# Other order of products, earlier block sums and stores on another queue in the up projections of a hybrid decoder trunk

## The chip, the cores and the metric

The kernel runs on one core of a Trainium2 chip. Its engines are TensorE (PE, matmuls; PEld is its weight load), VectorE (DVE), ScalarE (ACT), GpSimd (POOL) and SyncE (SP, which only issues DMAs here). Each engine takes its instructions in program order and waits at the first one that is not ready; DMAs are issued in that order as well, from SP's or ScalarE's queue. The metric is device microseconds of one execution, the median of three runs. The profile is one execution taken by the hardware profiler.

## What is computed

A trunk of two layers on 1024 tokens of width 1024, in float32. Layer 0 mixes with an S5 state space model and gated linear attention, layer 1 with an xLSTM matrix memory. Each mixer is followed by a gated MLP with a causal convolution of width 3, and the change lies in that MLP:

```python
def conv_ffn(h, w_up, conv_w, conv_b, w_down):
    g, u = jnp.split(h @ w_up, 2, axis=-1)          # 1024 -> 2 x 2816
    g = causal_dwconv(g, conv_w, conv_b)
    return ((jax.nn.gelu(g, approximate=True) * u) @ w_down).astype(h.dtype)

# per layer
x = x + rms_norm(mix, ln_mix_post[layer])
h = rms_norm(x, ln_ffn_pre[layer])
f = conv_ffn(h, ffn_w_up[layer], ffn_conv_w[layer], ffn_conv_b[layer], ffn_w_down[layer])
x = x + rms_norm(f, ln_ffn_post[layer])
```

## The kernel before, in words

Every large product is made in three matmuls: each operand is cut into a rounded part h (ScalarE copies it into the fast 32-bit format) and the remainder l (DVE subtracts), and TensorE adds hh, hl and lh (`cut`, `mm3`). Matmuls have 512 columns. A "product" below is one 512 x 128 output tile over half of the depth: 4 depth tiles x 3 matmuls = 12 matmuls.

The up projection works in 22 pairs j: 128 columns of g and the 128 columns of u beside them, for all 1024 tokens in two halves, lo and hi. Each pair is a 2 x 2 block product with 7 products instead of 8 (a Winograd form). Two of them ("11" and "21", `up_first`) need the lo tokens only and the plain weight block a (of g). Five (`up_pair`) need sums of weight blocks and the block sums T1 to T4 and "22" of the activations, which `prenorm_blocks` makes from both halves, in four steps c of transposes, DVE, ScalarE and POOL work. While the hi half is still being normed, the first `EARLY` = 10 pairs run `up_first` alone (the early loop of `ffn`); they store g and u of the lo half to DRAM in `first` and load them again later (`outputs`). So there are ten early pairs with 5 products left (60 matmuls) and twelve whole pairs with 7 (84 matmuls). Pair 0 is the first one after the early loop.

The weights come through `Stream`, a list of units. A unit loads raw blocks on SP's queue (tags wr for a, wq for b, three buffers each), makes its tensor and cuts it. `next` gives the weights of the next unit, `advance` cuts units up to two ahead and loads further ones if buffers are free; `hold` keeps it from loading wq blocks until the early loop is over. `up_units` lists them per pair: for a whole pair first the plain a, then "sums" (POOL makes four sums of 512 columns: d = a1 - b1, b1 += b2, a1 = b1 - a1, a2 -= a1, and a is cut), then b, then d. Products of a pair come as T2 (first half of the sums), T1 and T4 (b), 22 (second half of the sums), T3 (d).

After a pair, `gate` makes the convolution (first tap on POOL, two more taps on DVE) and GELU (ScalarE); `late`, called after T2 of the next pair, multiplies with u on DVE and stores the product to `md` on SP, then issues the loads of the next outputs. `od_prep` prepares the odd layer's block matrices in the background during layer 0's MLP (POOL, TensorE transposes, ScalarE copies). Background tasks are put between the matmuls by `tick`, which keeps a planned time per lane; `finish` puts the rest of a task at once. The order of instructions on each engine is the order of the program.

Of the kernel before, what the change touches and what calls it, by code (L numbers as in the profile page):

```python
# [8 lines left out]
F32 = mybir.dt.float32  # L9
# [16 lines left out]
class Unit:  # L26
# [4 lines left out]
    def __init__(self, loads, make=None, state=None, done=("a",), keep=0):  # L31
        self.loads, self.make, self.done, self.keep = loads, make, done, keep
        self.state = {} if state is None else state

# [5 lines left out]
class Stream:  # L40
# [29 lines left out]
    def _cut(self):  # L70
        u = self.units[self.n_cut]
        r = u.make(self.k, u.state)
# [17 lines left out]
    LOOK = 3  # L90

# [88 lines left out]
class Trunk:  # L180
# [157 lines left out]
    def prenorm_blocks(self, xt, ss, gain, layer, base, out):  # L338
# [21 lines left out]
        for c in range(4):  # L360
# [17 lines left out]
            V.tensor_tensor(out=t34[:, 1], in0=t12[:, 1], in1=h2, op=ALU.subtract)  # L378
            G.tensor_tensor(out=t34[:, 1], in0=t34[:, 1], in1=l2, op=ALU.subtract)
# [123 lines left out]
    EARLY = 10  # L503

    def up_units(self, w, pairs, early):

        def col(c0):  # L510
            return w[:, c0 : c0 + 128].rearrange("(k p) c -> p k c", p=128)

        def sums(k, s):
            G = k.nc.gpsimd
            k.ws.live["wq"] += 1
            s["d"] = k.ws.raw([128, 4, 128], "wq")
            (a1, a2), (b1, b2) = ((s[n][:, 0:4], s[n][:, 4:8]) for n in "ab")
            G.tensor_tensor(out=s["d"], in0=a1, in1=b1, op=ALU.subtract)
            G.tensor_tensor(out=b1, in0=b1, in1=b2, op=ALU.add)
            G.tensor_tensor(out=a1, in0=b1, in1=a1, op=ALU.subtract)  # L520
            G.tensor_tensor(out=a2, in0=a2, in1=a1, op=ALU.subtract)
            return s["a"]

        units = [plain(col(c0)) for c0, _ in pairs[:early]]
        for i, (c0, c1) in enumerate(pairs):
            s, a, b = {}, ("a", col(c0)), ("b", col(c1))
            if i >= early:
                units.append(Unit([a], lambda k, s: s["a"], s, ()))
            units += [
                Unit([b] if i >= early else [a, b], sums, s, ("a",), 1),  # L530
                Unit([], lambda k, s: s["b"], s, ("b",)),
                Unit([], lambda k, s: s["d"], s, ("d",)),
            ]
        return units
# [9 lines left out]

    def up_first(self, B, g, u):
# [4 lines left out]
        p = self.up_product(w, 1, B["21"])  # L550
        self.nc.vector.tensor_tensor(out=g, in0=u, in1=p, op=ALU.add)

    def up_pair(self, B, g, u, late):

        lo, hi = slice(0, HT), slice(HT, 2 * HT)
        product = self.up_product

        def acc(o, i, ps, op=ALU.add):
            self.nc.vector.tensor_tensor(out=o, in0=i, in1=ps, op=op)

        wa = self.ws.next()
        acc(u[:, lo], u[:, lo], product(wa, 0, B["T2"]))
        late()
        wb = self.ws.next()
        acc(u[:, hi], u[:, lo], product(wb, 0, B["T1"]))
        acc(u[:, lo], u[:, lo], product(wb, 1, B["T4"]), ALU.subtract)
        acc(g[:, hi], u[:, hi], product(wa, 1, B["22"]))
        p = product(self.ws.next(), 0, B["T3"])
        acc(u[:, hi], u[:, hi], p)
        acc(u[:, lo], u[:, lo], p)  # L570
# [103 lines left out]
    def ffn(self, layer, src, hT, nxt):  # L674
# [4 lines left out]
        B = {"11": hT[0][0][:4], "21": hT[0][0][4:]}  # L679
        for j in range(self.EARLY):  # L680
            st = self.ws.raw([128, 2, HT], "wq")
            self.up_first(B, st[:, 0], st[:, 1])
            nc.sync.dma_start(out=self.first[j], in_=st)
        self.hold = False
# [4 lines left out]
        def gate(j, g):  # L689
# [20 lines left out]
        pend = None  # L710
# [16 lines left out]
        for j in range(NF):  # L727
            g, u = nxt_out
            if j >= self.EARLY:
                self.up_first(B, g[:, lo], u[:, lo])  # L730
            if j + 1 == NF:
                self.mids_load(1)
            self.up_pair(B, g, u, late)
# [3 lines left out]
        product()  # L737

# [872 lines left out]
    def od_prep(self):  # L1611
# [15 lines left out]
        gout = pre.tile([128, self.NT, 8], F32, name="gout")  # L1627
        yield 60000
        for c2 in range(8):
# [13 lines left out]
            for i in range(3):  # L1643
# [3 lines left out]
                o = pre.tile([128, 2, 128], F32, tag=f"bt{i}", name=f"bt{i}")  # L1647
# [17 lines left out]
            nc.vector.tensor_copy(gout[:, cs], pg[:, 0])  # L1665
# [4 lines left out]
        nc.sync.dma_start(out=self.gxd, in_=gout)  # L1670
# [592 lines left out]
```

## Time and profile before

| | us |
|---|---|
| median of 3 runs | 2810.51 (2805.34 to 2813.19) |
| profiled execution | 2813.47 |
| its span, first to last instruction | 2811.5 |
| TensorE busy | 2651.5 (94%) |
| VectorE busy | 1699.8 (60%) |
| ScalarE busy | 1042.5 (37%) |
| GpSimd busy | 777.0 (28%) |

The profile's page gives busy time by engine, and a slice table with the clock that TensorE was granted (PEclk, 1.00 is the full 2.4 GHz). A matmul's shown duration includes the fill of the array, so matmuls overlap: the distance from one start to the next is what one costs. The timeline lists instructions in order of time with, in brackets, how long the engine had been idle and what ended it. The windows view gives busy time per engine, number of instructions, clock and DMA share for a stretch.

### The profile page before, as it was taken

The page shows a single profiled execution, that of the slowest core. Times are in us where ns is not written, and L with a number is a line of the kernel's source. Part 1 is how long each engine was busy: PE and PEld are TensorE (multiplying, and loading weights), DVE is VectorE, ACT ScalarE, POOL GpSimd, SP SyncE. Part 2 cuts the span into 40 slices and gives each one's busy share as a digit, 9 for nine tenths or more (in the row PEclk, how much of TensorE's full clock was granted, in tenths as well). Part 3 has the DMA queues.
Part 4 walks back from the last instruction along what each step waited for, and adds up shares of the span by engine and source line. Part 5 has one row for each costly group of instructions (what it writes and reads, how often), then busy time and mean ns, then how long its engine had stood idle before and what let it go on. Part 6 is the DMA issues. An engine that isn't in the chain of part 4 may idle for free. (4 is left out here: it accounts for less than half of the span.)

```text
span 2811.5 us, 34544 instructions
## 1 busy us (share of the span) xinstructions
PE 2651.5 (94%) x13102; PEld 2193.7 (78%) x13102; DVE 1699.8 (60%) x2333; ACT 1042.5 (37%) x1580; POOL 777.0 (28%) x763
## 2 busy tenths in 40 slices
PE   6899899799999999999999999999997999999997
PEld 5676678677788788878788799998785777878886
DVE  7576456767656644377266467764556776666453
ACT  4233644422222333355344544433433222223331
POOL 2832003455343101020000035550113643330021
PEclk9999999899999999999999999999998999999999
DMA  5544446434232455265445534435444342325552
GB/s 139 151 132 128 139 139 190 155 107 145 80 98 71 147 183 202 91 200 157 135 146 157 177 122 141 135 101 194 167 169 138 120 135 75 90 68 202 180 194 75
DMA packets 413682, 392.10 MB, mean 139 GB/s; under 512 B 57902, under 2 KB 319624, under 8 KB 413388
## 3 DMA queue, kind: packets, MB, share of 16 engines
q1 hardware_dynamic: 374268, 354.69, 39.9%
q10 hardware_dynamic: 39248, 35.20, 3.6%
q8 instruction: 103, 1.69, 0.2%
q14 instruction: 63, 0.52, 0.1%
HBM read 288.96 MB, written 98.78 MB: 138 GB/s over the span
## 5 line engine op out<-in xcount | busy, mean ns | idle before, releaser
L118 DVE TENSOR_TENSOR wl<-wr,wh 128x1024 fp32r<-128x1024 f32 (+1 forms) x323 | 405.2, 1256 | 669.2 <-ACT wh L118 657.5
L134 PE MATMUL ps<-hh,wh 128*128 128x512 f32 x1876 | 750.2, 400 | 19.1 <-ACT wh L118 14.9
L134 PE MATMUL ps<-hh,wl 128*128 128x512 f32 x1876 | 742.8, 396 | 13.4 <-DVE wl L118 11.2
L134 PE MATMUL ps<-hl,wh 128*128 128x512 f32 x1876 | 739.1, 394 | 0.9 <-DVE hl L118 0.9
L118 ACT ACTIVATE wh<-wr 128x1024 fp32r<-128x1024 f32 (+1 forms) x326 | 338.9, 1041 | 699.3 <-PE ps L134 476.0
L134 PEld LDWEIGHTS ps<-hh,wl 128*128 128x128 f32 x1876 | 355.4, 189 | 106.3 <-DVE wl L118 28.0
L134 PEld LDWEIGHTS ps<-hh,wh 128*128 128x128 f32 x1876 | 356.5, 190 | 103.1 <-ACT wh L118 18.4
L134 PE MATMUL ps<-wh,hh 128*128 128x512 f32 x1076 | 423.9, 394 | 2.9 <-ACT hh L118 1.7
L134 PE MATMUL ps<-wh,hl 128*128 128x512 f32 x1076 | 420.1, 390 | 1.6 <-DVE hl L118 1.6
L134 PE MATMUL ps<-wl,hh 128*128 128x512 f32 x1076 | 419.9, 390 | 0.8 <-DVE wl L118 0.8
L134 PEld LDWEIGHTS ps<-hl,wh 128*128 128x128 f32 x1876 | 356.5, 190 | 74.7 <-DVE hl L118 1.4
L134 PEld LDWEIGHTS ps<-wh,hh 128*128 128x128 f32 x1076 | 202.6, 188 | 47.5 <-ACT hh L118 2.8
L134 PEld LDWEIGHTS ps<-wh,hl 128*128 128x128 f32 x1076 | 202.5, 188 | 45.5 <-DVE hl L118 2.9
L134 PEld LDWEIGHTS ps<-wl,hh 128*128 128x128 f32 x1076 | 202.7, 188 | 42.2 <-DVE wl L118 1.1
L118 POOL TENSOR_TENSOR rsp<-ms,mhalf 128x4 f32<-128x4 f32 x8 | 8.1, 1014 | 564.1 <-DVE ms L118 564.1
L118 DVE TENSOR_TENSOR wl<-wq,wh 128x1024 fp32r<-128x1024 f32 x88 | 107.4, 1220 | 88.5 <-ACT wh L118 88.5
L118 ACT ACTIVATE xs<-xs 128x1024 f32<-128x1024 f32 x44 | 46.7, 1062 | 258.8 <-DVE xs L118 212.5
L118 DVE TENSOR_TENSOR ys<-ys,ps 128x512 f32<-128x512 f32 x207 | 137.6, 681 | 4.6 <-PE ps L134 3.2
L118 POOL TENSOR_SCALAR xs<-xs,par_t 128x256 f32<-128x256 f32 (+1 forms) x96 | 100.9, 1061 | 118.1 <-DVE xs L118 118.1
L118 DVE SCALAR_TENSOR_TENSOR xs<-xs,par_t 128x1023 f32<-128x1023 f32 x88 | 126.9, 1442 | 1.6
L118 POOL TENSOR_TENSOR wq<-wr,wq 128x512 f32<-128x512 f32 x44 | 59.2, 1346 | 200.7 <-DVE wl L118 149.5
L118 POOL TENSOR_TENSOR wr<-wq,wr 128x512 f32<-128x512 f32 x44 | 67.4, 1533 | 105.4 <-DVE wl L118 103.7
(394 smaller groups left out, 4039.7 us busy)
## 6 DMA issues: line engine op xcount, KB each, us to landing
wr<-in_ffn_w_down_dram SPq DMA_DIRECT2D x88, 512.0 KB, 3.7
wr<-in_ffn_w_up_dram SPq DMA_DIRECT2D x64, 512.0 KB, 4.8
wr<-in_od_w_in_dram SPq DMA_DIRECT2D x64, 512.0 KB, 3.9
wq<-in_ffn_w_up_dram SPq DMA_DIRECT2D x44, 512.0 KB, 5.7
md<-xs SPq DMA_DIRECT2D x44, 512.0 KB, 2.9
wq<-md SPq DMA_DIRECT2D x44, 512.0 KB, 4.8
wr<-in_od_w_out_dram SPq DMA_DIRECT2D x32, 512.0 KB, 3.6
wr<-in_ev_w_in_dram SPq DMA_DIRECT2D x28, 512.0 KB, 4.2
```

Source lines behind the costliest of these rows:

```text
L118: return f(*args, **kw)
L134: self.eng.matmul(out=out, lhsT=lhsT, rhs=rhs, start=start, stop=stop)
```

## The change

The order of the five products becomes T2, T3 (both with d), T1, T4 (both with b), 22 (with a2); T3 and T4 change sign in `prenorm_blocks`. The sums tile d now holds both a1 - b1 and b1 + b2 - a1 in a wq buffer of its own; three POOL sums come ahead of its cut and the fourth (a2) gets a unit of its own, `last`. A unit may be marked `ahead`: `prepare`, called after the T3 product and once in the early loop, loads and sums the next pair's blocks before their cut is due. `EARLY` is 14. The early loop keeps its results in two tiles `su` and `sg` of one buffer each and stores them from ScalarE's queue, `hold` is cleared ahead of it. In `gate` the first tap moves from POOL to ScalarE, and the store of the product of the pair before is issued there from ScalarE's queue instead of SP's. `od_prep` uses one tile less and shares two tags.

```diff
+    def prepare(self):
+        for n in range(self.n_cut, min(self.n_cut + 4, len(self.units))):
+            u = self.units[n]
+            if u.ahead and u.made is None:
+                while self.n_dma <= n:
+                    self._load(True)
+                u.made = u.make(self.k, u.state)
+                return
...
-    EARLY = 10
+    EARLY = 14
...
         def sums(k, s):
             G = k.nc.gpsimd
             k.ws.live["wq"] += 1
-            s["d"] = k.ws.raw([128, 4, 128], "wq")
-            (a1, a2), (b1, b2) = ((s[n][:, 0:4], s[n][:, 4:8]) for n in "ab")
-            G.tensor_tensor(out=s["d"], in0=a1, in1=b1, op=ALU.subtract)
+            d = s["d"] = k.ws.raw([128, 8, 128], "wq")
+            a1, b1, b2 = s["a"][:, 0:4], s["b"][:, 0:4], s["b"][:, 4:8]
+            G.tensor_tensor(out=d[:, 4:8], in0=a1, in1=b1, op=ALU.subtract)
             G.tensor_tensor(out=b1, in0=b1, in1=b2, op=ALU.add)
-            G.tensor_tensor(out=a1, in0=b1, in1=a1, op=ALU.subtract)
-            G.tensor_tensor(out=a2, in0=a2, in1=a1, op=ALU.subtract)
-            return s["a"]
+            G.tensor_tensor(out=d[:, 0:4], in0=b1, in1=a1, op=ALU.subtract)
+            return d
+
+        def last(k, s):
+            a2 = s["a"][:, 4:8]
+            k.nc.gpsimd.tensor_tensor(out=a2, in0=a2, in1=s["d"][:, 0:4], op=ALU.subtract)
+            return a2
...
-                Unit([b] if i >= early else [a, b], sums, s, ("a",), 1),
+                Unit([b] if i >= early else [a, b], sums, s, (), 1, True),
                 Unit([], lambda k, s: s["b"], s, ("b",)),
-                Unit([], lambda k, s: s["d"], s, ("d",)),
+                Unit([], last, s, ("a", "d")),
...
+        if whole:
+            acc(g[:, lo], u[:, lo], self.up_first(B, u[:, lo]))
+        w = self.ws.next()
+        acc(g[:, hi], u[:, lo], product(w, 0, B["T2"]))
+        p = product(w, 1, B["T3"])
+        self.ws.prepare()
+        acc(u[:, lo], g[:, hi], p)
         late()
+        w = self.ws.next()
+        p = product(w, 0, B["T1"])
+        acc(u[:, hi], u[:, lo], p)
+        acc(g[:, hi], g[:, hi], p)
+        acc(u[:, lo], u[:, lo], product(w, 1, B["T4"]))
+        acc(g[:, hi], g[:, hi], product(self.ws.next(), 0, B["22"]))
...
+        self.hold, before = False, None
+
+        def put(i, n, t):
+            nc.scalar.dma_start(out=self.first[i, :, n], in_=t)
+
         for j in range(self.EARLY):
-            st = self.ws.raw([128, 2, HT], "wq")
-            self.up_first(B, st[:, 0], st[:, 1])
-            nc.sync.dma_start(out=self.first[j], in_=st)
-        self.hold = False
+            u = self.fpool.tile([128, HT], F32, tag="su", name="su", bufs=1)
+            p = self.up_first(B, u)
+            if before:
+                put(j - 1, 0, before)
+            put(j, 1, u)
+            before = self.fpool.tile([128, HT], F32, tag="sg", name="sg", bufs=1)
+            nc.vector.tensor_tensor(out=before, in0=u, in1=p, op=ALU.add)
+            if j + 2 == self.EARLY:
+                self.ws.prepare()
+        put(j, 0, before)
...
-            nc.gpsimd.tensor_scalar(
-                out=tt, in0=g, scalar1=w[2], scalar2=self.par("ffn_conv_b", layer * NF + j), op0=ALU.mult, op1=ALU.add
+            nc.scalar.activation(
+                out=tt, in_=g, func=AF.Identity, scale=w[2], bias=self.par("ffn_conv_b", layer * NF + j)
             )
...
+            if done:
+                nc.scalar.dma_start(out=self.md[done[0] * 128 : (done[0] + 1) * 128], in_=done.pop())
+                done.clear()
             nc.scalar.activation(out=tt, in_=tt, func=AF.Gelu_apprx_tanh)
...
-            nc.sync.dma_start(out=self.md[i * 128 : (i + 1) * 128], in_=tt)
+            done.extend((i, tt))
```

## Rows read from the trace of the kernel before

**Rows 1.** The page, busy time of each engine over the whole span.

```profile
PE 2651.5 (94%) x13102; PEld 2193.7 (78%) x13102; DVE 1699.8 (60%) x2333; ACT 1042.5 (37%) x1580; POOL 777.0 (28%) x763
```

**Rows 2.** Windows, layer 1: early loop, pair 0, pairs 1 to 9, pairs 10 to 21.

```profile
core 0: us, PE busy (x) PEld busy (x) DVE busy (x) ACT busy (x) POOL busy (x), PEclk, DMA share, GB/s
2083.36:2146.92 63.56, 58.15 (x273) 48.27 (x271) 43.07 (x44) 27.72 (x42) 24.70 (x14) 0.99 0.45 158
2146.92:2178.65 31.73, 19.72 (x61) 14.21 (x61) 25.26 (x25) 11.88 (x15) 13.64 (x9) 0.64 0.42 133
2178.65:2317.21 138.56, 129.76 (x542) 102.17 (x540) 105.32 (x107) 32.54 (x36) 75.64 (x44) 0.98 0.41 125
2317.21:2555.87 238.66, 232.40 (x1010) 188.18 (x1008) 162.72 (x172) 65.31 (x76) 77.79 (x59) 1.00 0.30 91
```

**Rows 3.** Windows, layer 0: the same four stretches.

```profile
472.93:537.48 64.55, 58.83 (x273) 48.56 (x272) 45.14 (x46) 27.69 (x42) 26.97 (x17) 0.98 0.57 164
537.48:570.03 32.55, 21.75 (x82) 16.70 (x83) 24.30 (x23) 12.70 (x18) 18.73 (x13) 0.67 0.41 133
570.03:712.31 142.28, 135.69 (x607) 110.25 (x606) 106.77 (x115) 36.53 (x49) 82.79 (x54) 0.98 0.42 130
712.31:962.00 249.69, 243.24 (x1098) 198.86 (x1096) 159.21 (x178) 70.06 (x92) 86.91 (x69) 0.99 0.30 91
```

**Rows 4.** Windows, layer 1, single pairs: two early ones (1 and 6), a whole one.

```profile
2178.65:2192.25 13.60, 13.60 (x62) 11.26 (x60) 10.52 (x11) 4.88 (x5) 8.11 (x5) 1.00 0.12 40
2252.56:2269.10 16.54, 14.25 (x61) 10.92 (x59) 11.15 (x13) 2.69 (x4) 8.44 (x5) 1.00 0.57 177
2378.51:2398.21 19.70, 19.34 (x86) 15.69 (x84) 13.40 (x14) 5.12 (x7) 6.71 (x6) 1.00 0.28 81
```

**Rows 5.** Timeline, layer 1, ahead of pair 0: SP, POOL, ACT, PE; start, duration.

```profile
2111.62 19.87 SPq L683 DMA_DIRECT2D first<-wq  x4
2132.06 0.93 SPq L65 DMA_DIRECT2D wq<-in_ffn_w_up_dram  x1
...
2138.50 1.29 POOL L118 TENSOR_TENSOR wq<-wr,wq 128x512 f32<-128x512 f32 x1 [6.84 <-DMA wq<-in_ffn_w_up_dram]
...
2142.57 1.26 POOL L118 TENSOR_TENSOR wr<-wr 128x512 f32<-128x512 f32 x1
...
2143.86 1.06 ACT L118 ACTIVATE wh<-wr 128x1024 fp32r<-128x1024 f32 x1 [15.10 <-POOL wr L118]
...
2146.92 0.80 PE L134 MATMUL g<-hh,wh 128*128 128x512 f32 x1 [5.41 <-ACT wq L118]
2147.51 0.63 PE L134 MATMUL g<-hl,wh 128*128 128x512 f32 x1
```

**Rows 6.** Timeline, layer 1: transposes of blocks 0 and 1, last cut of block 0.

```profile
2111.92 0.60 PE L138 MATMUL ps<-ident,x 128*128 128x128 f32 x4
...
2123.01 1.04 PE L138 MATMUL ps<-ident,x 128*128 128x128 f32 x8
...
2121.96 1.23 DVE L118 TENSOR_TENSOR hl<-ys,hh 128x1024 fp32r<-128x1024 f32 x1 [0.26 <-ACT hh L118]
```

**Rows 7.** Timeline, layer 1, early pairs: taps on DVE twice, POOL's sum, DVE's wait.

```profile
2242.49 4.53 DVE L118 SCALAR_TENSOR_TENSOR xs<-xs,par_t 128x1023 f32<-128x1023 f32 x2
...
2257.15 2.60 DVE L118 SCALAR_TENSOR_TENSOR xs<-xs,par_t 128x1023 f32<-128x1023 f32 x2
2261.46 1.78 DVE L118 TENSOR_TENSOR wl<-wq,wh 128x512 fp32r<-128x512 f32 x1 [1.71 <-ACT wh L118]
...
2243.79 2.15 POOL L118 TENSOR_TENSOR wq<-wq 128x512 f32<-128x512 f32 x1
```

**Rows 8.** Issue to landing: early stores (line 683, SP); 256 KB stores (line 823, ScalarE).

```profile
DMA to landing us min/median/max: 2.6/3.4/5.9
...
DMA to landing us min/median/max: 1.6/2.1/3.6
```

**Rows 9.** Timeline, layer 0: an Identity with a per-partition operand on ScalarE.

```profile
136.25 0.69 ACT L118 ACTIVATE ze<-ps,par_t 128x512 f32<-128x512 f32 x1 [3.32 <-PE ps L134]
```

More of the change, by code (lines that the diff above doesn't have):

```diff
@@ L26, with __init__ @@
 class Unit:
-    def __init__(self, loads, make=None, state=None, done=("a",), keep=0):
-        self.loads, self.make, self.done, self.keep = loads, make, done, keep
+    def __init__(self, loads, make=None, state=None, done=("a",), keep=0, ahead=False):
+        self.loads, self.make, self.done, self.keep, self.ahead = loads, make, done, keep, ahead
         self.state = {} if state is None else state
+        self.made = None
 def plain(ap):
@@ L71, in _cut @@
         u = self.units[self.n_cut]
-        r = u.make(self.k, u.state)
+        r = u.make(self.k, u.state) if u.made is None else u.made
         h = self.k.wpool.tile(list(r.shape), F32R, tag="wh", name="wh", bufs=self.CUT)
@@ L377, in prenorm_blocks @@
             V.tensor_tensor(out=t12[:, 1], in0=b[:, 1], in1=t12[:, 0], op=ALU.subtract)
-            V.tensor_tensor(out=t34[:, 1], in0=t12[:, 1], in1=h2, op=ALU.subtract)
-            G.tensor_tensor(out=t34[:, 1], in0=t34[:, 1], in1=l2, op=ALU.subtract)
+            V.tensor_tensor(out=t34[:, 1], in0=h2, in1=t12[:, 1], op=ALU.subtract)
+            G.tensor_tensor(out=t34[:, 1], in0=t34[:, 1], in1=l2, op=ALU.add)
             h, l = pair()
@@ L543, in up_product, with up_first @@
         return ps
-    def up_first(self, B, g, u):
+    def up_first(self, B, u):
         w = self.ws.next()
@@ L549, in up_first, with up_pair, acc @@
         self.nc.scalar.activation(out=u, in_=p, func=AF.Copy)
-        p = self.up_product(w, 1, B["21"])
-        self.nc.vector.tensor_tensor(out=g, in0=u, in1=p, op=ALU.add)
-    def up_pair(self, B, g, u, late):
+        return self.up_product(w, 1, B["21"])
+    def up_pair(self, B, g, u, whole, late):
         lo, hi = slice(0, HT), slice(HT, 2 * HT)
         product = self.up_product
[L558 to L562, printed above, removed]
-        late()
[L564 to L570, printed above, removed]
+        def acc(o, i, ps):
+            self.nc.vector.tensor_tensor(out=o, in0=i, in1=ps, op=ALU.add)
+        if whole:
[5 more added lines that the diff above has]
+        acc(u[:, lo], g[:, hi], p)
+        late()
+        w = self.ws.next()
[4 more added lines that the diff above has]
+        acc(g[:, hi], g[:, hi], product(self.ws.next(), 0, B["22"]))
     def ffn_units(self, layer):
@@ L708, in outputs @@
             return g, u
-        pend = None
+        pend, done = None, []
         def product():
@@ L728, in ffn @@
             g, u = nxt_out
-            if j >= self.EARLY:
-                self.up_first(B, g[:, lo], u[:, lo])
             if j + 1 == NF:
                 self.mids_load(1)
-            self.up_pair(B, g, u, late)
+            self.up_pair(B, g, u, j >= self.EARLY, late)
             if j + 1 == NF:
@@ L737, in ffn @@
         product()
+        nc.sync.dma_start(out=self.md[done[0] * 128 : (done[0] + 1) * 128], in_=done[1])
         def more(half):
@@ L1626, in od_prep @@
             )
-        gout = pre.tile([128, self.NT, 8], F32, name="gout")
         yield 60000
@@ L1646, in od_prep @@
                     nc.tensor.transpose(ps[:, t], bd[i][:, t], self.ident)
-                o = pre.tile([128, 2, 128], F32, tag=f"bt{i}", name=f"bt{i}")
+                o = pre.tile([128, 2, 128], F32, tag=f"bd{i}", name=f"bt{i}")
                 yield 700
@@ L1664, in od_prep @@
             nc.scalar.dma_start(out=self.amat[:, cs], in_=o)
-            nc.vector.tensor_copy(gout[:, cs], pg[:, 0])
+            nc.vector.tensor_copy(wg[:, 0, cs], pg[:, 0])
             o = pre.tile([128, 2, 8], F32, tag="gv", name="gv")
@@ L1669, in od_prep @@
             yield 8000
-        nc.sync.dma_start(out=self.gxd, in_=gout)
+        nc.sync.dma_start(out=self.gxd, in_=wg[:, 0])
     def od_load(self):
```

## Prediction

> **What bounds the kernel now.** TensorE is busy for 2651.5 of 2811.5 us [rows 1], so only time in which it waits or runs slowly can be won. I read the windows first, one per stretch, with borders at the first matmul of each product group. The up stage takes 472.51 us in layer 1 [rows 2] and 489.07 us in layer 0 [rows 3]. A clean early pair is 60 matmuls in 13.60 us [rows 4], so a matmul costs 0.2267 us and the stage's 22 x 84 = 1848 matmuls cost 418.9 us. With 3.5 us for the four transpose groups (about 0.9 us net each, [rows 6]) layer 1 loses 50 us. Layer 0 has the same stage plus the preparation of the odd layer, and is 16.6 us longer; I keep that difference as it is.
>
> Where the 50 us lie in layer 1 [rows 2]: the early loop takes 63.56 us for 240 matmuls (54.4) and pair 0 takes 31.73 us for 60 (13.6), so 27.3 us, 24 without the transposes, lie at the border. Pairs 1 to 9 take 138.56 us for 122.4: 16.2 lost. Pairs 10 to 21 take 238.66 for 228.5: 10.2 lost, 0.66 in nearly every one (19.70 for 19.04, [rows 4]).
>
> The border, read in the timeline of four queues [rows 5]: SP is held for 19.87 us over four early stores, each waiting for a DVE sum; the load of pair 0's second block stands behind them and is issued at 2132.06. POOL gets it at 2138.50, its four sums end at 2143.83, and ScalarE, which wants the cut of those sums next, has by then waited 15.10 us. Behind that cut in ScalarE's order stand a PSUM copy and the cuts of the T blocks, so TensorE stops for 5.41 us [rows 5], and in pair 0 it is busy for 19.72 of 31.73 us only, 12 idle [rows 2]. After the first stop a matmul takes 0.63 us [rows 5], and pair 0 has a granted clock of 0.64 [rows 2]: much of it ran at 1.2 instead of 2.4 GHz. Idle and slow clock together are the 24.
>
> **Part 1, the early loop and the border.** Fourteen pairs give 336 matmuls, 76.1 us, plus 3.5 for transposes: 79.6. The T blocks: transposes of block 0 at 2111.92, of block 1 at 2123.01, 11.1 apart, and the last cut of block 0 ends at 2123.19, 11.3 after its transposes [rows 6]. At that pace block 3 starts at 2145.2 and is cut at 2156.5, while the loop ends at 2083.36 + 79.6 = 2163.0. So the four added pairs cover the blocks by 6 us. `hold` is cleared ahead of the loop and SP no longer carries the stores, so pair 0's second block is loaded ahead. Its cut is issued in iteration 12, and behind three POOL sums (3 x 1.29 to 2.15, 4 to 6.5 us, [rows 5, 7]) ends some 3 us before it is needed. `prepare` in iteration 12 then starts pair 1's sums: that tile takes the ring slot of pair 0's second block, so POOL waits there for that block's cut, and the one remaining subtraction of pair 0 queues behind it; it is wanted four products (10.9 us) later, which hides it.
>
> New cost: `su` and `sg` have one buffer. DVE's sum of iteration j rewrites `sg`, so it waits until the store of iteration j-1 has landed, and that store is issued only after ScalarE's copy of j. Other ScalarE stores of 256 KB land 2.1 us after issue (1.6 to 3.6), the early stores of before 3.4 (2.6 to 5.9) [rows 8]. Copy 0.6, other ScalarE work W between, 2.1 to land: the sum can run 2.7 + W after the copy began, and its product is there after 2.72. So DVE waits W. ScalarE is busy 27.72 of 63.56 us [rows 2], 2.4 us per 5.44 us iteration, so W lies between 0 and 2.4; I take 1. Behind the waiting sum on DVE stand the next weight cut and the T block work. DVE is busy 43.07 us of this stretch, nearly all ahead of the 15 us stop, so about 0.5 us per iteration is free. Over the eight iterations with T blocks in them (4 x 11.1 / 5.44) that is 8 x 0.5 = 4, plus 1 elsewhere: 5 us (0.5 to 15). Early loop: 84.6 us.
>
> **Part 2, fourteen early pairs.** The loads now run a pair ahead, since SP no longer waits at the product store, and the sums start when the block before is cut; the waits for sums (16.54 us in one pair, [rows 4]) should go. Next is DVE's own order. In pairs 1 to 9 it is busy 105.32 us, 11.7 a pair [rows 2]. In each pair it waits 1.71 us for GELU and the cut behind it [rows 7], which stays. New: the first tap of the convolution moves from POOL (the sums' engine) to ScalarE and now depends on the last product of the pair, so DVE waits for it with nothing else in hand: 1.06 to 1.2 us (a 512-column Identity took 0.69, [rows 9]; a 1024-column cut behind POOL 1.06, [rows 5]); I take 1.2. One POOL pass per pair less takes back about 0.3 of contention. 11.7 + 1.7 + 1.2 - 0.3 = 14.3 us against TensorE's 13.6: DVE sets the pace. 14 x 14.3 = 200.2 us; bounds 13.6 (DVE's lag hidden by weights cut ahead) and 15.4 (138.56 / 9, no better than now).
>
> Contention in the rows: the two taps on DVE took 2.60 us in one pair and 4.53 in another, where POOL's sums ran beside and took 2.15 instead of 1.29 [rows 5, 7]. The Trainium skill, page "SBUF — State Buffer", section "Who interferes with whom", says more: a DVE instruction with two SBUF inputs and a GpSimd instruction that reads SBUF exclude each other, the second one blocked in full. By that, four POOL passes of 1.29 could each add 1.29 to DVE, an estimate of 5.2 us a pair. The trace agrees that they collide, not that one is blocked in full: a stretch of 1.9 in the worst pair, both engines slowed. I keep the measured 11.7. The change speaks for more overlap than before: the sums are released at the end of the pair before, when the taps run.
>
> **Part 3, eight whole pairs.** The second block's cut stands behind GELU in ScalarE's order; it is wanted now after 11, 21, T2 and T3, 10.9 us, before after 11, 21 and T2, 8.2. That is 2.7 more for a wait that cost 0.66. DVE needs 13.4 + 2.9 = 16.3 of 19.04 [rows 4]. So 8 x 19.04 = 152.3, plus 1 for what is left (0 to 5.3).
>
> **Parts at nothing.** 49 stores a layer (21 products, 28 early halves) are now issued by ScalarE; even at 0.93 us, the longest issue in [rows 5], that is 46 us in a stage in which it is busy for 137 of 472 [rows 2], hidden, and 46 a layer if it all stood on the path. Four more extra loads of 512 KB and as many stored and reloaded: the DMA share is 0.41 to 0.45 here. The gate of the last pair starts one product later, hidden by the down products that need earlier tiles first; else 2.7. The shared tags in the preparation: the copy waits for transposes that fill its own source.
>
> **Sum.** Layer 1: 84.6 + 200.2 + 153.3 = 438 for 472.5, 34.5 less. Layer 0 adds 16.6 to both: the same 34.5. Together 69. The profiled run took 2813.47 us (span 2811.5 and 2 around it), 3 above the median of 2810.51: 2813.5 - 69 - 3 = 2741.5, so 2742.
>
> **Rivals.**
> - DVE and POOL collide more. If the taps always take 4.53, about 1 us over the mean in the 11.7, an early pair takes 15.3: 14 x 1 x 2 = 28 more, 2770. For: the sums now start beside the taps. Against: one POOL pass fewer. If each of the four passes held DVE for its whole 1.29 us, that is 5.2 a pair, of which the 11.7 hold about 1.2: 2742 + 28 x 4 = 2854. DVE's busy time with five passes beside it speaks against that: 0.02. This is the exclusion that the Trainium skill states in that section of "SBUF — State Buffer".
> - The sums are not sooner where it matters: pair 0's cut still blocks ScalarE and the 24 us stay in each layer, a gain of about 21, 2789. For: POOL still does the T blocks' work ahead of them. Against: the load is no longer behind 19.87 us of waits. 0.08.
> - Slower: the store round trip in the early loop. Copy 0.6, W, landing, sum 0.7, then the copy again, since the sum reads `su`. With the longest early landing, 5.9, and W = 2.4 it is 9.6 us against 5.44: 14 x 4.2 = 58 a layer instead of the 5 counted, 2 x 53 more, 2848. It decides from 5.44 + (34.5 + 5) / 14 = 8.3 us an iteration; between about 8 and 8.6 it ends as no change. For: single buffers, and loads and stores share the DMA engines. Against: ScalarE's stores of this size landed in 1.6 to 3.6 us. 0.06 slower, 0.06 no change.
>
> **How the numbers follow.** Forecast (2712 to 2765) 0.64, collision (2765 to 2782) 0.14, sums not sooner 0.08, round trip 0.06 and 0.06, full exclusion 0.02. Faster 0.86, within 0.3% (8.4 us, about what can be told from no change) 0.06, slower 0.08. The bounds of the terms add up to 423 to 468 a layer, 2711 to 2801 in all, hardly all on one side; the range 2712 to 2790 leaves out the last three cases and little else, about 0.17.
>
> **What would show it.** Right: no ScalarE wait over 5 us ahead of pair 0, its window near 14 us at granted clock 1.0, early pairs near 14.3 with TensorE waiting for DVE cuts, whole pairs near 19.04. Wrong: early iterations well over 6 us with DVE idle on a landing store (round trip), early pairs over 15 (collision), a stop ahead of pair 0 (sums not sooner), or a table load beside each Identity, which the rows do not show.

## The result and the profile after

The changed kernel takes 2767.08 us (median of four runs, 2764.25 to 2771.23), the kernel before on the same chip 2809.5: a ratio of 0.9851, 95% interval 0.9831 to 0.987. That is 42 us less; the forecast was 2742, some 68 less. The profiled run of after has a span of 2769.2 us.

The windows view of after, layer 1, in the stretches of [rows 2]: early loop (14 iterations now), pair 0, the other early pairs (13), whole pairs (8). Columns as there.

```profile
2061.71:2148.36 86.65, 80.72 (x370) 66.14 (x368) 65.74 (x66) 41.07 (x60) 29.87 (x17) 1.00 0.58 187
2148.36:2164.28 15.92, 15.39 (x60) 12.33 (x61) 9.80 (x12) 4.73 (x6) 5.40 (x5) 0.89 0.53 179
2164.28:2358.95 194.67, 186.25 (x782) 143.94 (x781) 150.50 (x152) 64.03 (x66) 90.20 (x52) 1.00 0.41 134
2358.95:2513.75 154.80, 153.21 (x674) 125.89 (x673) 111.45 (x119) 53.58 (x59) 43.59 (x29) 1.00 0.28 90
...
2237.11:2252.32 15.21, 14.47 (x62) 11.03 (x60) 11.91 (x14) 4.83 (x5) 6.96 (x4) 1.00 0.42 139
...
2358.95:2380.47 21.52, 19.93 (x86) 15.53 (x85) 17.80 (x20) 6.26 (x7) 7.35 (x5) 1.00 0.26 82
2380.47:2399.51 19.04, 19.04 (x86) 15.77 (x85) 13.81 (x14) 6.38 (x7) 6.29 (x5) 1.00 0.26 84
```

The four stretches add up to 452.0 us for 472.5 before: 20.5 less in layer 1. In layer 0 the same sum is 464.9 for 489.1, 24.2 less. Together 44.7, so the whole gain (42.3 by the two spans) lies in these two stages. The last three lines are single pairs: an early one with 15.21 (the forecast had 14.3, TensorE's own time is 13.60), the first whole one with 21.52, and the second, clean with 19.04. Pair 0 went from 31.73 us at a clock of 0.64 [rows 2] to 15.92 at 0.89.

What is left of the stop ahead of pair 0 is in the timeline of ScalarE (ACT) and TensorE (PE):

```profile
2147.25 1.06 ACT L130 ACTIVATE wh<-wq 128x1024 fp32r<-128x1024 f32 x1 [3.81 <-POOL wq L130]
...
2148.36 0.50 PE L146 MATMUL g<-hh,wh 128*128 128x512 f32 x1 [3.71 <-ACT wh L130]
```

TensorE stands still for 3.71 us at the end of the loop, since ScalarE waits for POOL's sums of pair 0. The 2.3 us that pair 0 itself takes over 13.60 are 0.53 of waiting and a slow start: its first 5 us ran at a granted clock of 0.66.

One early pair of after in the timeline of VectorE (DVE), POOL and ScalarE, in order of time:

```profile
2240.00 1.22 DVE L130 TENSOR_TENSOR wl<-wq,wh 128x1024 fp32r<-128x1024 f32 x1
2241.13 0.68 DVE L130 TENSOR_TENSOR xs<-xs,ps 128x512 f32<-128x512 f32 x1
...
2241.35 1.29 POOL L130 TENSOR_TENSOR wq<-wr,wq 128x512 f32<-128x512 f32 x1 [8.11 <-DVE wl L130]
...
2241.85 1.25 ACT L130 ACTIVATE xs<-xs,par_t 128x1024 f32<-128x1024 f32 x1 [6.05 <-DVE xs L130]
...
2243.13 4.19 DVE L130 SCALAR_TENSOR_TENSOR xs<-xs,par_t 128x1023 f32<-128x1023 f32 x2 [1.31 <-ACT xs L130]
...
2244.09 2.15 POOL L130 TENSOR_TENSOR wq<-wq,wr 128x512 f32<-128x512 f32 x1
2246.20 2.27 POOL L130 TENSOR_TENSOR wr<-wr,wq 128x512 f32<-128x512 f32 x1
...
2247.41 1.06 ACT L130 ACTIVATE xs<-xs 128x1024 f32<-128x1024 f32 x1 [4.32 <-DVE xs L130]
2248.50 0.63 ACT L130 ACTIVATE wh<-wr 128x512 fp32r<-128x512 f32 x1
...
2249.16 0.69 DVE L130 TENSOR_TENSOR wl<-wr,wh 128x512 fp32r<-128x512 f32 x1 [1.85 <-ACT wh L130]
```

It is to be read twice. Along VectorE: the accumulation of 22 of the pair before, a wait of 1.31 for Identity, two taps in 4.19 (2.60 where nothing collides, [rows 7]), a wait of 1.85 for the cut of a2, which stands behind GELU. Busy 11.91, the two waits 3.16: the rest of the 15.21, 0.14, is short gaps. Along POOL: the first sum starts when VectorE has cut b (2241.2; the sums tile takes that block's ring slot), three sums and `last` end at 2248.47, and ScalarE cuts a2 at 2248.50. GELU, at the end of the other chain, ends at 2248.47 as well. Both chains reach ScalarE at the same time, so this profile alone can't say which one sets the pair. The experiments had to.

### The profile page after: what moved, and what is told of

Same layout as the page of the kernel before. It is cut to its first block, busy times and chain, and to the rows that moved or that the text cites. A ratio compares the mean times of both kernels' runs of the same rounds, so it can differ in the third digit from the quotient of the medians.

```text
span 2769.2 us, 34708 instructions
## 1 busy us (share of the span) xinstructions
PE 2641.8 (95%) x13102; PEld 2187.4 (79%) x13102; DVE 1702.7 (61%) x2333; ACT 1097.1 (40%) x1624; POOL 727.9 (26%) x719
## 4 chain that ended last, share of the span: by engine, by line
PE 65%; DVE 13%; POOL 8%; issue 6%; ACT 4%; DMA 4%; SPq 0%; ACTq 0%; DVEq 0%; POOLq 0%
PE ps L146 60%; PE g L146 4%; POOL wq L130 3%; DVE wl L130 3%; DVE xs L130 2%; DVE ys L130 1%; POOL wr L130 1%; PE ps L150 1%; POOL turn L130 1%; ACT wh L130 1%; DVE hl L130 1%; DVE num L130 1%; DMA wr<-in_ffn_w_up_dram 1%; POOL w1t L130 1%; DMA first<-sg 1%
## 5 line engine op out<-in xcount | busy, mean ns | idle before, releaser
L130 DVE TENSOR_TENSOR wl<-wr,wh 128x1024 fp32r<-128x1024 f32 (+1 forms) x323 | 384.2, 1191 | 558.5 <-ACT wh L130 549.4
L130 ACT ACTIVATE wh<-wr 128x1024 fp32r<-128x1024 f32 (+1 forms) x326 | 319.4, 982 | 411.8 <-PE ps L146 373.0
L146 PEld LDWEIGHTS ps<-hh,wh 128*128 128x128 f32 x1880 | 355.1, 189 | 91.3 <-ACT wh L130 11.7
L130 DVE SCALAR_TENSOR_TENSOR xs<-xs,par_t 128x1023 f32<-128x1023 f32 x88 | 165.0, 1874 | 56.8 <-ACT xs L130 55.2
L130 ACT ACTIVATE xs<-xs,par_t 128x1024 f32<-128x1024 f32 x44 | 54.8, 1246 | 185.4 <-DVE xs L130 185.4
L130 ACT ACTIVATE wh<-wq 128x1024 fp32r<-128x1024 f32 x88 | 90.8, 1050 | 87.0 <-PE ps L146 64.2
L130 POOL TENSOR_TENSOR wr<-wr,wq 128x512 f32<-128x512 f32 x44 | 76.4, 1738 | 123.8 <-DVE wl L130 123.8
```

The lines of the kernel that those rows point to most:

```text
L130: return f(*args, **kw)
L146: self.eng.matmul(out=out, lhsT=lhsT, rhs=rhs, start=start, stop=stop)
```

## The experiments

Each kernel is made from the changed kernel. The ratio is to the kernel before, on the same chip. The column of early pairs gives pairs 1 to 13 of layer 1 from the windows (13 x 13.60 is 176.8).

| | median us | ratio, 95% | pairs 1 to 13 |
|---|---|---|---|
| after | 2767.08 | 0.9851 (0.9831 to 0.987) | 194.67 |
| short_sums | 2730.39 | 0.972 (0.9697 to 0.9743) | 176.80 |
| sums_after_taps | 2774.4 | 0.9879 (0.9856 to 0.9901) | 198.15 |
| gate_spread | 2814.31 | 1.002 (1.0008 to 1.0032) | 220.90 |
| tap_pool | 2839.82 | 1.0113 (1.0086 to 1.014) | 228.65 |
| one_ahead | 2761.33 | 0.9831 (0.9817 to 0.9846) | 191.66 |
| one_fence | 2773.35 | 0.9873 (0.9853 to 0.9892) | 198.95 |
| one_spread | 2763.82 | 0.9843 (0.9826 to 0.9859) | 192.73 |
| two_sets | 2753.7 | 0.9802 (0.9785 to 0.982) | 195.58 |
| early10 (9 pairs) | 2785.48 | 0.991 (0.989 to 0.993) | 133.91 |
| md_sp | 2764.73 | 0.9839 (0.9823 to 0.9855) | 194.48 |
| best | 2726.43 | 0.9695 (0.9675 to 0.9715) | 184.53 |
| best_fetch | 2721.04 | 0.9681 (0.9663 to 0.9699) | 176.80 |

**short_sums.** Are POOL's sums behind the lost time at all? The kernel leaves out three quarters of each sum.

```diff
-            G.tensor_tensor(out=d[:, 4:8], in0=a1, in1=b1, op=ALU.subtract)
+            a1, b1, b2 = a1[:, 0], b1[:, 0], b2[:, 0]
+            G.tensor_tensor(out=d[:, 0], in0=a1, in1=b1, op=ALU.subtract)
...
-            return d
+            return s["a"]
```

> The four sums of POOL work on 128 of their 512 columns (three quarters of the block sums are left out and the plain block is cut in place of the sums tile); their order, their waits and the buffers stay. Theory (the sums, released by the cut of b, run over the two taps and stretch them from 2.60 to 4.19 us; VectorE sets the early pair): taps back to about 2.6 us, early pairs from 15.23 to about 13.6, 28 x 1.6 = 45 us less, about 2722. Rival (only the two waits of VectorE, 1.31 for Identity and 1.85 for the cut behind GELU, or late loads, set the pair): early pairs stay at 15.2, time within 8 us of 2767.

Measured: all thirteen early pairs run in 13.60, and the first whole pair in 19.04 instead of 21.52. The timeline of one pair, DVE and POOL:

```profile
2223.24 0.46 POOL L130 TENSOR_TENSOR wq<-wr,wq 128x128 f32<-128x128 f32 x1 [11.54 <-DVE wl L130]
...
2225.02 2.60 DVE L130 SCALAR_TENSOR_TENSOR xs<-xs,par_t 128x1023 f32<-128x1023 f32 x2 [1.31 <-ACT xs L130]
2229.33 0.69 DVE L130 TENSOR_TENSOR wl<-wr,wh 128x512 fp32r<-128x512 f32 x1 [1.71 <-ACT wh L130]
```

The taps are back at 2.60 while both waits of VectorE are still there, so the waits alone do not set the pair. The gain is 37 us and not 45: in layer 0 the thirteen pairs go from 205.69 to 189.79 only, because TensorE is busy for all of the 189.79, with the preparation's transposes among its work. But short sums shorten the chain along POOL as well as the taps. The result does not tell the two apart.

**sums_after_taps.** Moves the sums off the taps.

```diff
+            f = self.small.tile([128, 4], F32, tag="fence", name="fence", bufs=2)
+            nc.gpsimd.tensor_copy(f, tt[:, 2 * HT - 4 :])
             if done:
```

> A copy of 4 columns on POOL reads the output of the second tap, so the next sums start only when the taps are over. Theory that it is the taps (two SBUF inputs, 1023 columns) that collide with the sums: taps about 2.6 us, early pairs 13.6 to 14.2, 2722 to 2740. Variant, the collision only moves to the weight cuts and the accumulations that VectorE runs next: early pairs stay about 15.2, about 2767. If the sums then come too late for the cut of d, VectorE waits for POOL and early pairs are over 15.5, over 2775.

Measured: the pair grew from 15.23 to about 15.65, and the taps stayed at 4.19. The timeline of POOL and ScalarE says why:

```profile
2255.92 1.29 POOL L130 TENSOR_TENSOR wq<-wr,wq 128x512 f32<-128x512 f32 x1 [8.11 <-DVE wl L130]
...
2262.02 0.19 POOL L130 COPY fence<-xs 128x4 f32<-128x4 f32 x1 [1.21 <-DVE xs L130]
2262.16 1.29 POOL L130 TENSOR_TENSOR wr<-wr,wq 128x512 f32<-128x512 f32 x1
2262.24 1.06 ACT L130 ACTIVATE xs<-xs 128x1024 f32<-128x1024 f32 x1 [4.58 <-POOL fence L130]
...
2263.49 0.63 ACT L130 ACTIVATE wh<-wr 128x512 fp32r<-128x512 f32 x1 [0.19 <-POOL wr L130]
```

The expectation had the order on POOL wrong: the three sums that start there belong to a later pair and are already in the queue ahead of the copy; only `last` was held back. Two things lengthened the pair by 0.42. GELU rewrites the tile that the copy reads, so it starts 0.35 us behind the taps in place of 0.09; and the cut of a2 then waits another 0.19 for `last`. The second is a first, small sign of the chain along POOL.

**gate_spread.** Takes VectorE's two waits away by putting other work between.

```diff
         acc(g[:, hi], u[:, lo], product(w, 0, B["T2"]))
+        taps()
         p = product(w, 1, B["T3"])
+        gelu()
...
         acc(u[:, lo], u[:, lo], product(w, 1, B["T4"]))
+        mul()
```

> The gate is spread over the next pair: Identity where it was, the two taps behind the T2 accumulation, GELU behind the T3 product, the product with u behind the T4 accumulation. Theory (VectorE's in-order list with its two waits of 1.31 and 1.85 us sets the early pair): the waits go, VectorE is busy about 11.9 us a pair, TensorE sets the pace at 13.6, 28 x 1.6 = 45 us less, about 2722, even if the taps still collide with the sums. Rival (loads or the sums themselves come late): early pairs stay near 15.2, about 2767. Rival (the collision grows where the sums find more of VectorE's work beside them): VectorE busy over 13.6, early pairs 14 to 15, 2735 to 2760.

Measured: the opposite, 17.33 a pair and all of the gain gone. From the timeline, POOL, ScalarE and DVE:

```profile
2260.42 1.29 POOL L130 TENSOR_TENSOR wr<-wr,wq 128x512 f32<-128x512 f32 x1
...
2261.74 0.63 ACT L130 ACTIVATE wh<-wr 128x512 fp32r<-128x512 f32 x1 [3.56 <-POOL wr L130]
...
2262.41 0.69 DVE L130 TENSOR_TENSOR wl<-wr,wh 128x512 fp32r<-128x512 f32 x1 [5.51 <-ACT wh L130]
...
2263.61 2.60 DVE L130 SCALAR_TENSOR_TENSOR xs<-xs,par_t 128x1023 f32<-128x1023 f32 x2
```

Here nothing collides (taps 2.60, sums 1.29), and VectorE stands still for 5.51 us until the cut of a2 comes, which waits for `last`. The theory of VectorE's list alone fell with this run. The code gives the reason: `prepare` is called once in the early loop, so in pair j it already makes the sums of pair j+2. `last` of pair j+1 is issued after them, and they wait for VectorE's cut of b of pair j+1. So four POOL passes lie between that cut and the cut of a2 of the same pair, with two products (T1, T4) between them on TensorE, and VectorE's list leads from the cut of a2 back to the next cut of b. In after the taps lie beside these passes; gate_spread put them behind, into the loop.

**tap_pool.** The first tap back on POOL.

```diff
-            nc.scalar.activation(out=tt, in_=g, func=AF.Identity, scale=w[2], bias=...)
+            nc.gpsimd.tensor_scalar(out=tt, in0=g, scalar1=w[2], scalar2=..., op0=ALU.mult, op1=ALU.add)
```

> Only the first tap goes back to POOL, ahead of the sums. Theory: VectorE's wait for Identity (1.31 us) becomes a wait for a POOL pass of 1024 columns (about 2.2 us), and the sums still start over the taps: early pairs about 16, 28 x 0.9 = 25 us more, about 2790. Rival (the wait for the first tap is not on the path, the sums are): early pairs near 15.2 or below, 2767 or less.

Measured: 73 us more, three times what was expected. The wait of VectorE for the tap in one pair:

```profile
2307.14 3.61 DVE L130 SCALAR_TENSOR_TENSOR xs<-xs,par_t 128x1023 f32<-128x1023 f32 x2 [4.78 <-POOL xs L130]
```

Not one POOL pass but three sums and the tap (1.20 us) stand ahead of it. The wait is 3.5 us longer than the one for Identity, the taps 0.6 shorter. Of the parts taken back in these runs, the move of the tap to ScalarE is the one that the new `prepare` needs most; I had costed it as a loss of 1.2 us a pair.

**one_ahead.** `prepare` makes the sums of the next pair only, so `last` comes ahead of them.

```diff
-            if j + 2 == self.EARLY:
-                self.ws.prepare()
```

> The call of prepare in the early loop is left out, so prepare in pair j makes the sums of pair j+1 and no longer of j+2. Seen so far: spreading the gate took VectorE's waits away and the taps ran in 2.60 us, yet the early pair grew to 17.33, with the cut of a2 waiting for POOL each time. Theory B formed from that: the subtraction `last` of a pair stands on POOL behind the three sums of the next pair, and those wait for VectorE's cut of this pair's b; four passes, the cut of a2 and VectorE's way back to the next cut of b close a loop of 15.23 us. By B `last` now comes first, and early pairs fall to 13.6 to 14.2: 2722 to 2740. Theory A (VectorE's own list: taps stretched to 4.19, waits of 1.31 and 1.85 us): the sums still start when b is cut, over the taps, and the pair stays at 15.2, 2767.

Measured: 14.8 in most pairs, between the two. The ratios of after and of this kernel overlap; thirteen pairs are 3.0 us shorter in layer 1 and 4.9 in layer 0. The timeline, DVE, POOL and ScalarE:

```profile
2252.74 4.07 DVE L130 SCALAR_TENSOR_TENSOR xs<-xs,par_t 128x1023 f32<-128x1023 f32 x2 [1.31 <-ACT xs L130]
...
2255.81 2.16 POOL L130 TENSOR_TENSOR wr<-wr,wq 128x512 f32<-128x512 f32 x1
...
2256.91 1.06 ACT L130 ACTIVATE xs<-xs 128x1024 f32<-128x1024 f32 x1 [4.20 <-DVE xs L130]
2257.87 0.61 ACT L130 ACTIVATE wh<-wr 128x512 fp32r<-128x512 f32 x1
...
2258.52 0.69 DVE L130 TENSOR_TENSOR wl<-wr,wh 128x512 fp32r<-128x512 f32 x1 [1.71 <-ACT wh L130]
```

The cut of a2 starts at 2257.87, before the POOL pass beside it ends (2257.97; it is the `last` of the next pair): it no longer waits for POOL. What is left is VectorE's list: waits of 1.31 and 1.71, and 11.85 busy with taps of 4.07. So there were two loops of nearly the same length, and taking one away gives what the other one allows. Each theory alone was wrong.

**one_fence** is one_ahead with the copy of sums_after_taps.

> As one_ahead, and the next sums start only behind the two taps (a copy of 4 columns on POOL reads their output). Theory A and B together (both loops hold): the taps run in 2.60, VectorE's list is 10.3 busy plus 3.2 of waits = 13.5, and early pairs are 13.6: 2722. If a wait for the sums returns, early pairs are over 14.5, 2745 or more.

Measured: the taps are at 2.60, but the pair is 15.69. Now `last` and the sums do start behind the taps, and the cut of d waits for them:

```profile
2261.05 2.60 DVE L130 SCALAR_TENSOR_TENSOR xs<-xs,par_t 128x1023 f32<-128x1023 f32 x2 [1.31 <-ACT xs L130]
...
2269.58 2.01 ACT L130 ACTIVATE wh<-wq 128x1024 fp32r<-128x1024 f32 x2 [3.69 <-POOL wq L130]
```

The taps can be freed of the collision at the price of later sums, which costs more.

**one_spread** is one_ahead with the spread gate of gate_spread.

> As one_ahead, with the gate spread over the next pair as in gate_spread. Theory B: gate_spread was slow since the loop over POOL had the taps and GELU in it as well; with `last` ahead of the sums early pairs are 13.6, 2722. Rival (what made gate_spread slow is the ScalarE order, the cut of d behind GELU behind the taps): early pairs stay at 17.3, 2814.

Measured: 15.19 in most pairs. The 17.33 are gone, so the loop over POOL did cause them; but two waits are back on VectorE, at other places:

```profile
2237.32 0.69 DVE L130 TENSOR_TENSOR wl<-wr,wh 128x512 fp32r<-128x512 f32 x1 [1.83 <-ACT wh L130]
...
2243.70 1.22 DVE L130 TENSOR_TENSOR wl<-wq,wh 128x1024 fp32r<-128x1024 f32 x1 [1.53 <-ACT wh L130]
```

The cut of a2 now stands behind Identity (1.25) in ScalarE's order and the cut of d behind GELU, which waits for the taps.

**two_sets.** The early loop alone: a second place for its results. `hold` is cleared four iterations before the end instead of ahead of the loop, since the results now lie in the wq ring.

```diff
+            ring = j % 2 and j < self.EARLY - 4
+            if j == self.EARLY - 4:
+                self.hold = False
+            if ring:
+                st = self.ws.raw([128, 2, HT], "wq")
+                u = st[:, 1]
...
-            before = self.fpool.tile([128, HT], F32, tag="sg", name="sg", bufs=1)
+            before = st[:, 0] if ring else self.fpool.tile([128, HT], F32, tag="sg", name="sg", bufs=1)
```

> The early loop alone: the results of iterations 1, 3, 5, 7 and 9 go into a buffer of the wq ring instead of su and sg, so each sum of the first ten has a tile whose store is two iterations old. Theory (single buffers and the way to memory and back cost the early loop part of its 7 us over 79.6): VectorE's waits for a store go in the first ten iterations and the loop is 80 to 84 us, 6 to 10 us less in all, about 2759. Rival (the loop's excess comes from the T blocks' work on VectorE and ScalarE): 85 to 87 us, 2767.

Measured: the loop takes 79.80 us in layer 1, with TensorE busy all of it, and pair 0 takes 13.60. First the waits of DVE in the early loop of after, then the windows of two_sets (early loop and pair 0, layer 1; early loop, layer 0):

```profile
DVE sg L130 <- DMA first<-sg: 8.9, 4, 3.7
```

```profile
2056.31:2136.11 79.80, 79.80 (x369) 66.38 (x368) 66.97 (x67) 41.91 (x61) 29.98 (x17) 1.00 0.64 207
2136.11:2149.71 13.60, 13.60 (x61) 11.26 (x60) 7.62 (x11) 3.83 (x5) 5.11 (x4) 1.00 0.56 182
...
473.87:554.41 80.54, 80.54 (x376) 66.90 (x374) 69.16 (x67) 43.10 (x63) 35.84 (x23) 1.00 0.73 215
```

Four waits of VectorE for a store that has not landed, 8.9 us in sum, are gone. The single buffers cost 6.85 us in the loop of layer 1 (86.65 less 79.80) and 5.2 in layer 0 (85.74 less 80.54), and 2.3 and 0.5 more in pair 0.

More than half of the 6.85 is the one stop of 3.71 ahead of pair 0. The longest wait for a store (3.7 us, until 2134.05 in after) has the last T block's work behind it on VectorE. POOL does its part of that work ahead of pair 0's sums, and these start 80.2 us after the loop's start in after (2141.93) and 71.6 in two_sets (2127.90). In two_sets no wait of TensorE is left in the loop or in pair 0 of layer 1.

**early10.** What are the four added early pairs worth?

```diff
-    EARLY = 14
+    EARLY = 10
```

> The changed kernel with 10 early pairs in place of 14. An early pair and its early iteration cost 15.23 + 5.44 = 20.7 us where a whole pair costs 19.04, so four of them less save 6.5 us a layer; what they buy is cover for the T blocks, whose last cut was worked out 73 us after the loop's start, some 15 after a loop of ten iterations. Theory (the cover is worth more): a stop of about 15 us ahead of pair 0 returns, 5 to 12 us a layer in sum, 2777 to 2790. Rival (the border was helped by the earlier loads alone): no stop, 2754 to 2762.

Measured: the stop is back. Windows of layer 1 (early loop, pair 0, pairs 1 to 9, whole pairs), and the stop in the timeline of ScalarE and TensorE:

```profile
2074.21:2134.47 60.26, 58.37 (x273) 48.27 (x272) 44.39 (x46) 27.76 (x42) 23.41 (x13) 1.00 0.57 189
2134.47:2167.95 33.48, 17.14 (x63) 12.62 (x62) 24.40 (x24) 12.10 (x15) 14.16 (x9) 0.75 0.32 103
2167.95:2301.86 133.91, 128.44 (x542) 99.72 (x540) 102.95 (x104) 44.70 (x46) 61.50 (x36) 1.00 0.41 132
2301.86:2532.76 230.90, 229.38 (x1010) 188.96 (x1008) 164.29 (x175) 79.12 (x87) 67.79 (x45) 1.00 0.27 88
```

```profile
2129.66 1.06 ACT L130 ACTIVATE wh<-wq 128x1024 fp32r<-128x1024 f32 x1 [6.91 <-POOL wq L130]
...
2140.23 0.50 PE L146 MATMUL g<-hh,wh 128*128 128x512 f32 x1 [4.14 <-ACT hh L130]
```

Loop and pair 0 are 93.7 us for 95.3 before [rows 2], although the loads are early here: TensorE waits for the T blocks (hh), not for pair 0's weights. But ScalarE still stood for 6.91 us at the cut of pair 0's sums, with cuts of T blocks behind it (15.10 in [rows 5]). So the earlier loads and sums do not win the border without the cover; whether fourteen pairs win it without them was not run. The four pairs are worth 17 us of the whole, net, by the ratios (0.991 less 0.9851). Most of the other 25 lies in pairs 1 to 9 (133.91 for 138.56) and whole pairs (230.90 for 238.66), in layer 0 in whole pairs nearly alone (241.40 for 249.69; pairs 1 to 9 took 140.95 for 142.28). How much of it the new order of products brings and how much `prepare` was not run.

**md_sp.** The stores of the products back to SP's queue.

```diff
-            done.extend((i, tt))
+            nc.sync.dma_start(out=self.md[i * 128 : (i + 1) * 128], in_=tt)
```

> Only the stores of the products to md go back to the queue of SP, issued right behind the product. Theory (SP waits at the store for the product, and the loads of b and a of a later pair stand behind it, but they run a pair ahead now): early pairs 15.2 to 15.6, 2767 to 2778. Rival (the gain of the change came from taking the stores off SP): loads late, waits for sums return, early pairs 16 or more, over 2789.

Measured: no difference that can be told, 194.48 us for the thirteen pairs. The queue of the products' stores is worth nothing here.

**best.** one_ahead and two_sets, and a gate whose steps stand behind the cuts in ScalarE's order.

```diff
+        p = product(w, 0, B["T2"])
+        first()
+        acc(g[:, hi], u[:, lo], p)
         p = product(w, 1, B["T3"])
         self.ws.prepare()
         acc(u[:, lo], g[:, hi], p)
+        taps()
         late()
...
         acc(g[:, hi], g[:, hi], p)
+        gelu()
         acc(u[:, lo], u[:, lo], product(w, 1, B["T4"]))
+        p = product(self.ws.next(), 0, B["22"])
+        mul()
+        acc(g[:, hi], g[:, hi], p)
```

> As one_ahead and two_sets together, with the gate spread otherwise than in one_spread, where VectorE still had 3.4 us of waits a pair, since the cut of a2 stood behind Identity and the cut of d behind GELU in ScalarE's order. Here Identity is issued behind the cut of a2, the taps behind the T3 accumulation, GELU behind the cut of d, the product with u ahead of the 22 accumulation. Theory (early pairs are set by VectorE's in-order list: 11.8 busy with the collision in it, plus its waits): the waits go, early pairs are 13.6, 28 x 1.6 = 45 us less, and 13 less in the early loops as in two_sets: about 2709. Rival (POOL's sums, late by the load of b or by collisions, are next): early pairs 14.5 to 15, 2735 to 2753.

Measured: between theory and rival. Pairs 1 to 4 run in 13.60 (four, where the next expectation says six), the later ones in 13.9 to 14.8, with the first sum waiting for a load. POOL's waits in pairs 1 to 13 of layer 1 (us in all, times, longest):

```profile
POOL wq L130 <- DMA wq<-in_ffn_w_up_dram: 68.4, 8, 13.4
```

**best_fetch.** The load of the pair after the next goes ahead of the outputs' loads, which wait for the taps.

```diff
         self.ws.prepare()
+        self.ws.fetch()
         acc(u[:, lo], g[:, hi], p)
```

> As best, where six early pairs of layer 1 ran in 13.60 and the others in 14.2 to 14.8, with the first sum waiting for the load of b; that load stands on SP behind the loads of the next outputs, which wait for the taps. Here the a and b of the pair after the next are loaded ahead of those outputs. Theory (SP's order makes the sums late): the sums start on VectorE's cut of b or earlier, early pairs of layer 1 are 13.6 throughout, 8 us less than best, about 2718. Rival (with the waits gone VectorE's own list, 12 us and more beside the sums, or ScalarE's, is the limit): no change to best, 2726.

Measured: 2721.04 us, 3.2% less than before. The windows of layer 1, in the same four stretches, and VectorE's longest group of waits in pairs 1 to 13 (us in all, times, longest):

```profile
2034.79:2114.59 79.80, 79.80 (x369) 66.38 (x368) 67.27 (x66) 42.29 (x61) 32.08 (x18) 1.00 0.64 207
2114.59:2128.40 13.81, 13.81 (x62) 11.19 (x61) 10.61 (x12) 3.60 (x5) 11.27 (x8) 1.00 0.54 179
2128.40:2305.20 176.80, 176.80 (x782) 146.44 (x781) 158.13 (x155) 67.03 (x67) 83.18 (x49) 1.00 0.46 149
2305.20:2457.52 152.32, 152.32 (x674) 126.17 (x673) 101.66 (x114) 55.53 (x59) 48.29 (x28) 1.00 0.27 89
```

```profile
DVE ys L138 <- PE ps L154: 11.6, 11, 2.0
```

TensorE is busy for the whole of the stage, 422.7 us for 418.9 of matmuls and the transposes. VectorE is busy for 158.13 us in the thirteen pairs, 7.6 more than in after, and this costs nothing: the collision lengthens its work still, but what it waits for now is TensorE's products, and TensorE waits for nothing.

## Why the prediction came out as it did

The sign, the place and the range held; the gain was 42 instead of 68. The range held because it took in a rival: 2767 lies outside the forecast's own 2712 to 2765, in the band of the collision (2765 to 2782, a chance of 0.14). The prediction's own signs say the same: whole pairs are at 19.04, but early pairs are over 15, and pair 0 is not near 14 at a clock of 1.0. By the terms of the sum, layer 1, forecast and measured: early loop 84.6 and 86.65; early pairs 200.2 and 210.6 (15.92 + 194.67); whole pairs 153.3 and 154.80; together 438 and 452. In layer 0 the forecast was 438 + 16.6 = 454.6 and the measured sum is 464.9. The two differences, 14 and 10, are nearly all of what was missing. Three quarters of the 14 is one term, the early pairs.

**The early pair, 14.3 forecast, 15.23 measured.** The waits were sized well: 1.7 for GELU and the cut became 1.85, 1.2 for Identity became 1.31. The busy time was not: 11.7 less 0.3 of contention was put in, 11.91 was measured, since the sums start with the cut of b and so lie over the taps in every pair that VectorE paces (4.19, in [rows 7] once 2.60, once 4.53). That is 0.5 of the 0.9 missing; the waits are 0.3 and gaps 0.1. The step that failed is the one that took the mean of before and gave back 0.3 for the missing POOL pass; the sentence after it, that the change speaks for more overlap, was right and was left to the rival. That rival named 15.3 a pair and 2770.

**The rival's number was right, its mechanism half.** A second loop of the same length stood behind VectorE's list: `last` behind the three sums of a later pair. The prediction saw this queueing for pair 0 and hid it behind "four products (10.9 us)". In the pairs that follow, VectorE cuts b late, and the four passes (7.1 us) with the cut of a2 and VectorE's list back to the next cut of b close a loop: the cut of a2 on VectorE starts 9.2 us after that of b (2249.16, 2240.00), the next cut of b 6.1 later (2255.23). The sum had no term for this. gate_spread showed that loop, one_ahead took it away and showed the other. What the collision alone costs is not settled: every kernel that took it off the taps moved the sums as well (short_sums shortened them, one_fence delayed them). That it sets no limit by itself is shown by best_fetch.

**The form of the collision.** Taken one by one, the two taps and POOL's passes of that pair of after take turns. The pass ahead of those shown above, and the two taps:

```profile
2242.72 1.29 POOL L130 TENSOR_TENSOR wq<-wq 128x512 f32<-128x512 f32 x1
2243.13 1.96 DVE L130 SCALAR_TENSOR_TENSOR xs<-xs,par_t 128x1023 f32<-128x1023 f32 x1 [1.31 <-ACT xs L130]
2245.12 2.19 DVE L130 SCALAR_TENSOR_TENSOR xs<-xs,par_t 128x1022 f32<-128x1022 f32 x1
```

The pass ends at 2244.01, the first tap at 2245.09, the third sum at 2246.24, the second tap at 2247.31, `last` at 2248.47: 1.07 to 1.16 us apart, each a little less than such an instruction takes alone (1.28 and 1.29). So each waited until the other engine's instruction was over, and the longer durations hold that wait. The longer taps of [rows 7], one by one, each end 1.1 behind a pass as well (2244.79 behind 2243.70, 2247.02 behind 2245.94). The prediction read them as both engines slowed and argued from that against a full exclusion; this reading was wrong. The ends show the exclusion, and what was wrong is its price: 2854 let each of four passes hold VectorE for its whole 1.29 us, where two taps waited for the rest of one pass each, 1.6 us a pair together. Two passes waited for the taps, 1.8 us together, so the collision lengthens both loops. By the Trainium skill, page "SBUF — State Buffer", section "Who interferes with whom", one of the two engines is blocked in full for each overlap. The trace agrees, by these ends.

**The early loop, 84.6.** The mechanism (the sum waits for a store two halves back, with the T blocks' work behind it) was right and its size near: 5 us forecast, 6.85 and 5.2 measured by two_sets. It came as four waits and not as one in each iteration, and it made pair 0's sums late, where the prediction had their cut done 3 us early: hence the stop of 3.71 and the 2.3 more in pair 0, which the sum did not have. The slower rival built on it did not come near: the longest wait was 3.7 us, and not in every iteration.

**The border.** Of the 24 us some 15 were won; the other 9 are the single buffers' (6.85 and 2.3). Fourteen early pairs do cover the T blocks: after has no stop at them. That the earlier load of pair 0's block wins the border by itself is not borne out: early10 has that load early and still stops. "Sums not sooner" did not come in its size (2789), but its mechanism is there: POOL does the T blocks' work ahead of pair 0's sums, and the cut of these holds ScalarE for 3.81 us in after and 6.91 in early10.

**Whole pairs, parts at nothing.** Seven of eight are clean at 19.04; the first one loses 2.5 where 1 was put in for all. The products' stores on ScalarE cost nothing and bring nothing (md_sp); the early halves' stores were not put back. Layer 0 was taken as layer 1 plus 16.6; it is 12.8 in after and 20.6 in best_fetch, where nothing but TensorE's own work is left. That part of the preparation's work had run in TensorE's waits before would explain it; no run takes the preparation out to show it.

## What to carry to other kernels

When a step is prepared further ahead, look at what is issued behind it on the same engine: a short operation that is wanted soon (here `last`) then waits for work that is wanted late and is itself held by a ring slot. When an engine's list shows busy time and waits that add up to the period, look for a second loop of the same length before paying for the first: here a repair of one loop alone brought 6 us or less (one_ahead) or cost time (gate_spread), and both repaired, with the order of ScalarE and SP and 13 us from the second buffer, brought 46. And two buffers in place of one are cheap where a ring is idle at that time: 13 us here without more memory.

## What was not expected of the hardware

The accumulations on VectorE that read one operand from PSUM took 0.67 to 0.69 us beside POOL's passes and without them. Those with both operands from SBUF took longer beside such a pass, each by a wait for the other engine's instruction: the subtraction of a weight cut 1.22 to 2.31 (one_spread), the taps 2.60 to 4.19, and POOL's pass 1.29 to 2.15 to 2.27 at the same time. An Identity with 1024 columns and per-partition operands took 1.25 us on ScalarE, and no table load appeared between it and GELU after the first one of the stage.
